# The head of a one-core decoder layer: the values' projection goes first, by rows, and A's chunks run on normed rows

## The chip, the cores and the metric

The kernel runs on one core of one Trainium2 chip. The metric is the device time of one execution in microseconds (us), taken as the median of several runs. Engines are named as in the profile: PE (TensorE's matmuls), PEld (its weight loads), DVE (VectorE), ACT (ScalarE), POOL (GpSimd) and SP (SyncE, which issues nearly all DMAs here).

## The reference

One layer over 256 rows of 1024 channels, all in float32:

```
hn  = rmsnorm(x, norm_mix)                      # per row: x * rsqrt(mean(x^2) + eps) * g
aq, ak, av, bq, bkc, ..., cq, ck, cv, mg = split(hn @ w_in)
o_a = dilated attention of A (6 heads);  o_b = sparse attention of B;  o_c = attention of C
x   = x + (sum of sigmoid(mg) * (o @ w_branch)) @ w_out
x   = x + conv_ffn(rmsnorm(x, norm_ffn));  out = rmsnorm(x, norm_final)
```

Only the first two lines are touched: the norm of `x` and the projections that give A's queries and keys (`aq`, `ak`) and the values `av` of A and `bvs` of B.

## The kernel before, in words

Every large product is made of float32r matmuls on parts: a weight is loaded as `raw` and split into `whi` (a rounded copy, on ACT) and `wlo` (the difference, on DVE or POOL), the activations likewise, and hi*hi, hi*lo and lo*hi are summed in PSUM. Weights come in "units" of up to 128x2048 values (1 MB), in the order of `_unit_list`; each is one DMA on SP's queue (two for the first ones), into one of four `raw` buffers, and its parts go into one of two pairs of `whi`/`wlo` buffers. SP issues in program order and waits at a load whose buffer is still in use.

The work has a head that is written out by hand (`tc.manual_schedule`: ACT, DVE, POOL and PE keep the order of the code), and then a part that a list scheduler orders engine by engine. In the head before:

- `x` is loaded as two tiles of 128 rows, then `table`, then the units a0 and a1 in halves and a2 whole. Nine small matmuls (`keep_warm`, L288) keep PE busy until `x` is there.
- `turn(t)` (L284) transposes x's tile t on PE, 8 blocks of 128x128; both tiles of a block of channels lie side by side, so what is made from `xT` needs both tiles. A small product with `table` (L332) makes the bias table, which goes through DRAM into `T`.
- `hi_part`, `lo_part` (L314, L316, L319) give the parts `x_hi`, `x_lo` of the weighted but not yet normed rows, 256 wide. Chunk c of A's queries and keys (a0, a1, a2 hold two chunks each) is the weights' 128 columns as the stationary operand and `x_hi`/`x_lo` as the moving one: 24 matmuls of 256 columns (L325 for a0, `chunk3_T` L298/L300 for the rest). The row's factor (`rows_m`) is multiplied in afterwards (`by_rows_rstd`, L292).
- Meanwhile ACT and DVE make the normed rows `whole` and their parts `h_parts` (`hn`: hi and lo side by side, 512 wide; L386 to L396), on which everything later works.
- After the head come unit kvc (two chunks by `chunk3_T`, 48 matmuls of 256 columns, L298/L300), then `proj_V("v1")`: rows of h as the stationary operand, the weights (512 columns) as the moving one, 48 matmuls (L238 to L240), copied to `V1` by DVE (L457). Then A's scores (L508) and softmax (L515 to L590), B's queries (`chunk_T`, L426/L428), A's output and so on.

## Time and profile before

| | |
|---|---|
| time, median of 3 runs | 424.87 us (424.62 to 425.62) |
| the profiled execution | 424.76 us, of which the span from first to last instruction is 423.0 |
| PE busy | 412.4 us, 98% of the span |
| DVE, ACT, POOL busy | 313.2 us (74%), 256.2 us (61%), 18.3 us (4%) |
| DMA | 78.00 MB, mean 184 GB/s |
| granted TensorE clock, mean | 0.996 |

Instructions are timed from the start of the span. A row of the timeline gives start, duration, engine, source line, operation, output and input, count, and in brackets how long the engine had been idle before it and what it had waited for. Matmuls overlap: one of 256 columns is shown as some 283 ns long, while the next begins 0.12 us after it, so the pace is read from starts.

### The profile page before, as it was taken

Reading aid. Unit: us, or ns where it says so; the run is one execution under the profiler, and the core shown is the slowest. Engines: PE = TensorE matmul, PEld = TensorE weight load, DVE = VectorE, ACT = ScalarE, POOL = GpSimd, SP = SyncE. Lnnn points to the kernel's source line nnn. Section 1 sums busy time; section 2 is a strip of 40 time slices with the busy share of each in tenths; the row PEclk is TensorE's granted clock in tenths of the full one; section 3 lists DMA queues with packets and bytes.
Section 4 is the critical chain, followed back from the end, with each engine's and each line's share of the span. In section 5 each row is a group of like instructions: output and inputs, shape, how many; then the busy total and the mean of one; then the engine's idle time right before and its main releaser. Section 6 shows DMA issues by size and latency. Waiting matters only on the chain.

```text
span 423.0 us, 6337 instructions
## 1 busy us (share of the span) xinstructions
PE 412.4 (98%) x2407; PEld 347.8 (82%) x2407; DVE 313.2 (74%) x624; ACT 256.2 (61%) x451; POOL 18.3 (4%) x28
## 2 busy tenths in 40 slices
PE   8999999999999999999999999999999999999993
PEld 7998778776667888878788998988888888888883
DVE  3996653788784888434753899998797797887765
ACT  5843283547787855555434889467476576584633
POOL 2500010120000000000000000000000000000001
PEclk9999999999999999999999999999999999999998
DMA  8999419532227793645350465565652743800002
GB/s 279 416 375 407 146 34 354 198 131 100 101 100 248 292 381 109 229 184 198 107 192 0 149 253 198 200 251 200 245 212 105 283 187 110 299 0 2 0 2 99
DMA packets 12750, 78.00 MB, mean 184 GB/s; under 512 B 1408, under 2 KB 1424, under 8 KB 4912
## 3 DMA queue, kind: packets, MB, share of 16 engines
q1 hardware_dynamic: 12144, 75.48, 47.8%
q0 software_dynamic: 576, 2.12, 1.4%
q8 instruction: 19, 0.31, 0.3%
q14 instruction: 11, 0.09, 0.1%
HBM read 76.52 MB, written 1.07 MB: 183 GB/s over the span
## 4 chain that ended last, share of the span: by engine, by line
PE 82%; DVE 8%; ACT 5%; DMA 2%; issue 2%; SPq 0%; POOLq 0%; POOL 0%; ACTq 0%
PE g L988 12%; PE g L239 10%; PE g L240 10%; PE g L238 10%; PE g L990 6%; PE acc L238 6%; PE acc L240 6%; PE acc L239 6%; PE g L298 3%; DVE wlo L226 2%; PE g L888 2%; PE o L541 2%; DMA raw<-in_wts_dram 2%; PE g L426 2%; PE g L300 1%
## 5 line engine op out<-in xcount | busy, mean ns | idle before, releaser
L226 DVE TENSOR_TENSOR wlo<-raw,whi 128x1024 fp32r<-128x1024 f32 (+2 forms) x131 | 154.1, 1201 | 41.0 <-ACT whi L222 40.6
L222 ACT ACTIVATE whi<-raw 128x1024 fp32r<-128x1024 f32 (+2 forms) x130 | 130.2, 1040 | 50.5 <-PE g L240 34.3
L988 PE MATMUL g<-parts,whi 128*128 128x512 f32 x256 | 89.4, 396 | 0.0
L990 PE MATMUL g<-parts,wlo 128*128 128x256 f32 x256 | 66.2, 279 | 0.0
L988 PEld LDWEIGHTS g<-parts,whi 128*128 128x128 f32 x256 | 46.7, 188 | 9.2
L990 PEld LDWEIGHTS g<-parts,wlo 128*128 128x128 f32 x256 | 48.2, 188 | 2.8
L239 PE MATMUL g<-wlo,hn 128*128 128x512 f32 (+1 forms) x128 | 50.0, 391 | 0.0
L240 PE MATMUL g<-whi,hn 128*128 128x512 f32 (+1 forms) x128 | 50.0, 391 | 0.0
L238 PE MATMUL g<-whi,hn 128*128 128x512 f32 (+1 forms) x128 | 49.8, 390 | 0.0
L967 DVE SCALAR_TENSOR_TENSOR cy<-xn,small_b,cy 128x255 f32<-128x255 f32 (+1 forms) x88 | 41.5, 480 | 9.0 <-ACT cy L965 8.0
L238 PE MATMUL acc<-whi,fl 128*128 128x512 f32 (+1 forms) x88 | 34.2, 389 | 0.1
L239 PE MATMUL acc<-wlo,fh 128*128 128x512 f32 (+1 forms) x88 | 34.0, 386 | 0.0
L240 PE MATMUL acc<-whi,fh 128*128 128x512 f32 (+1 forms) x88 | 34.0, 386 | 0.0
L965 ACT ACTIVATE cy<-xn,small_b 128x256 f32<-128x256 f32 x44 | 25.8, 598 | 7.4 <-DVE xn L997 7.4
L239 PEld LDWEIGHTS g<-wlo,hn 128*128 128x128 f32 x128 | 24.1, 188 | 5.1 <-issue 0.9
L240 PEld LDWEIGHTS g<-whi,hn 128*128 128x128 f32 x128 | 24.1, 188 | 4.2 <-issue 0.2
L238 PEld LDWEIGHTS g<-whi,hn 128*128 128x128 f32 x128 | 24.1, 189 | 4.0 <-ACT whi L222 0.2
L426 PE MATMUL g<-hn,whi 128*128 128x512 f32 x72 | 26.2, 405 | 0.0
L996 ACT ACTIVATE xn<-g 128x256 f32<-128x256 f32 x32 | 12.2, 380 | 22.2 <-PE g L988 22.2
L428 PE MATMUL g<-hn,wlo 128*128 128x256 f32 x72 | 19.9, 292 | 0.0
L997 DVE TENSOR_TENSOR xn<-g,xn 128x256 f32<-128x256 f32 x32 | 13.5, 421 | 8.3 <-ACT xn L996 8.3
L240 PEld LDWEIGHTS acc<-whi,fh 128*128 128x128 f32 x88 | 16.5, 188 | 3.4
(213 smaller groups left out, 698.6 us busy)
## 6 DMA issues: line engine op xcount, KB each, us to landing
raw<-in_wts_dram SPq DMA_DIRECT2D x61, 1024.0 KB, 4.8
gl<-in_w_dram SPq DMA_DIRECT2D x8, 512.0 KB, 7.6
raw<-in_wts_dram SPq DMA_DIRECT2D x5, 512.0 KB, 7.4
raw<-in_wts_dram SPq DMA_DIRECT2D x2, 804.0 KB, 9.0
T<-tvd POOLq DMA_DIRECT2D x1, 1280.0 KB, 16.3
xs<-in_x_dram SPq DMA_DIRECT2D x2, 516.0 KB, 3.8
out_dram<-raw SPq DMA_DIRECT2D x4, 256.0 KB, 2.1
T<-tvd POOLq DMA_DIRECT2D x1, 768.0 KB, 9.6
```

The costliest lines, as they stand in the source:

```text
L222: nc.scalar.activation(self.parts[0][:, sl], self.raw[:, sl], AF.Copy)
L226: return (eng or nc.vector).tensor_sub(self.parts[1][:, sl], self.raw[:, sl], self.parts[0][:, sl].bitcast(F32))
L238: nc.tensor.matmul(ps, al, bh, start=start, stop=False)
L239: nc.tensor.matmul(ps, ah, bl, start=False, stop=False)
L240: nc.tensor.matmul(ps, ah, bh, start=False, stop=stop)
L426: hi = lambda: nc.tensor.matmul(ps, view(0, k), h_parts[:, k].rearrange("p a q -> p (a q)"), start=k == 0, stop=k == KC - 1)
L428: lo = lambda: nc.tensor.matmul(ps[:, :S], view(1, k), h_hi[:, k, :], start=False, stop=False)
L965: on_act.append(nc.scalar.activation(y, u, AF.Identity, bias=vec_c[:, 3, ch:ch + 1], scale=vec_c[:, 2, ch:ch + 1]))
L967: nc.vector.scalar_tensor_tensor(y[:, sh:], u[:, :S - sh], vec_c[:, w, ch:ch + 1], y[:, sh:], op0=ALU.mult, op1=ALU.add)
L988: hi = lambda: nc.tensor.matmul(ps, u[0][:, k, cols], h_parts[:, k].rearrange("p a q -> p (a q)"), start=k == 0, stop=k == KC - 1)
L990: lo = lambda: nc.tensor.matmul(ps[:, :S], u[1][:, k, cols], h_parts[:, k, 0, :], start=False, stop=False)
L997: nc.vector.tensor_add(v, ps[:, :S], part)
```

## The change

The values' units v10 and v11 come first. SP loads x's first tile, then the first half of v10, then x's second tile, `table`, the other half of v10, v11, a0, a1, a2. The transposes of a tile are kept together (`turned[t]`: two PSUM tiles of four channel blocks each), so that the first tile's parts need the first tile alone. `weighted` (DVE, from PSUM, with the weights of the norm) writes `whole`, from which ACT makes `raw_hi` and DVE `raw_lo`. `value_products` multiplies rows of the weighted x by the weights, and the row's factor is applied when ACT copies the sums to `V1`. A's six chunks now wait for the normed parts `h_parts` and take 8 matmuls of 512 columns (hi of the weights on hi and lo of h) and 8 of 256 (`chunk_products`), whose halves `chunk_sum` adds. `keep_warm` runs 7 times ahead of the first transposes and 4 times (PAUSE) behind them. `proj_V("v1")` behind kvc is gone. No unit is split on POOL any more.

```diff
-WARM = 9
+WARM = 7
+PAUSE = 4
...
-    out = [(f"a{i}", "w_in", rows, [(C_AQ + 256 * i, 256)]) for i in range(3)]
+    out = [(f"v1{i}", "w_in", [(512 * i, 512)], [(C_AV, 384), (C_BVS, 128)]) for i in range(2)]
+    out += [(f"a{i}", "w_in", rows, [(C_AQ + 256 * i, 256)]) for i in range(3)]
     out.append(("kvc", "w_in", rows, [(C_BKC, 256)]))
-    out += [(f"v1{i}", "w_in", [(512 * i, 512)], [(C_AV, 384), (C_BVS, 128)]) for i in range(2)]
...
     psg = ctx.enter_context(tc.tile_pool(name="psg", bufs=2, space=bass.MemoryType.PSUM))
 
     xs = act_pool.tile([P, NT, D + KC], F32, name="xs")
-    for t in range(NT):
+
+    def load_x(t):
         nc.sync.dma_start(xs[:, t, :], x[t * P:(t + 1) * P, :])
+
+    load_x(0)
...
                 nc.sync.dma_start(self.raw[:, sl], src[:, sl])
+                if between and i == 0:
+                    between()
...
-    turned = [p.tile([P, 512], F32, name=n).rearrange("p (c q) -> p c q", c=2)
-              for p, n in ((ps_t, "t"), (ps_t, "t"), (ps_o, "o"), (ps_o, "o"))]
-    xT = [turned[c // 2][:, c % 2, :] for c in range(KC)]
+
+    whole = [mix.tile([P, 4, S], F32, name="gl", bufs=4) for _ in range(2)]
+
+    turned = [[p.tile([P, 512], F32, name=n).rearrange("p (c q) -> p c q", c=4) for _ in range(2)]
+              for p, n in ((ps_t, "t"), (ps_o, "o"))]
...
 
     T = qkv.tile([P, 16, 256], F32, name="T")
-    u_a0 = Unit("a0", cuts=2)
-    u_a1 = Unit("a1", cuts=2)
-    u_a2 = Unit("a2")
+
+    def load_rest():
+        load_x(1)
+        nc.sync.dma_start(tb, table)
+
+    u_v = [Unit("v10", cuts=2, between=load_rest), Unit("v11")]
     HALF = [slice(n * 512, (n + 1) * 512) for n in range(2)]
-    a0_ps = [psg.tile([P, 512], F32, name="g")[:, :S], s_tile()[:, 0, :S]]
+    V1_ps = [psg.tile([P, 512], F32, name="g"), s_tile()[:, 0, :]]
+    V1 = qkv.tile([P, NT, 512], F32, name="V1")
...
+        def weighted(t, i):
+            nc.vector.tensor_mul(whole[i][:, :, t * P:(t + 1) * P], turned[t][i],
+                                 g_mix[:, 4 * i:4 * i + 4, None].to_broadcast([P, 4, P]))
+
+        def raw_hi_part(t, i):
+            sl = slice(t * P, (t + 1) * P)
+            nc.scalar.activation(raw_hi[:, 4 * i:4 * i + 4, sl], whole[i][:, :, sl], AF.Copy)
+
+        def raw_lo_part(t, i):
+            sl = slice(t * P, (t + 1) * P)
+            nc.vector.tensor_sub(raw_lo[:, 4 * i:4 * i + 4, sl], whole[i][:, :, sl],
+                                 raw_hi[:, 4 * i:4 * i + 4, sl].bitcast(F32))
+
+        def value_products(t, ks, part):
+
             for k in ks:
-                for c, ps in enumerate(a0_ps):
-                    nc.tensor.matmul(ps, u_a0.views[part][:, k, c * P:(c + 1) * P], b[:, k, :],
-                                     start=part == 0 and b is x_hi and k == 0, stop=part == 1 and k == KC - 1)
+                u = u_v[k // 4]
+                for a in (raw_hi, raw_lo)[:2 - part]:
+                    nc.tensor.matmul(V1_ps[t], a[:, k, t * P:(t + 1) * P], u.views[part][:, k % 4, :],
+                                     start=part == 0 and a is raw_hi and k == 0, stop=part == 1 and k == KC - 1)
+
+        def normed_rows(i):
+            nc.vector.tensor_mul(whole[i], whole[i], rows_m[:, None, :].to_broadcast([P, 4, S]))
+
+        def normed_hi(i):
+            nc.scalar.activation(h_parts[:, 4 * i:4 * i + 4, 0, :], whole[i], AF.Copy)
+
+        def normed_lo(i):
+            sl = slice(4 * i, 4 * i + 4)
+            nc.vector.tensor_sub(h_parts[:, sl, 1, :], whole[i], h_parts[:, sl, 0, :].bitcast(F32))
+
+        def chunk_products(u, c):
+
+            ps = psg.tile([P, 512], F32, name="g")
+            cols = slice(c * P, (c + 1) * P)
+            for k in range(KC):
+                nc.tensor.matmul(ps, u.views[0][:, k, cols], h_parts[:, k].rearrange("p a q -> p (a q)"),
+                                 start=k == 0, stop=False)
+            for k in range(KC):
+                nc.tensor.matmul(ps[:, :S], u.views[1][:, k, cols], h_hi[:, k, :], start=False, stop=k == KC - 1)
+            return ps
+
...
+        def chunk_sum(ps):
+            j = len(aT)
+            scale = 0.125 if j < 3 else 1.0
+            part = halves[j % 2][:, :S]
+            nc.scalar.activation(part, ps[:, S:], AF.Copy, scale=scale)
+            aT.append(qkv.tile([P, S], F32, name=f"aT{j}"))
+            nc.vector.scalar_tensor_tensor(aT[j], ps[:, :S], scale, part, op0=ALU.mult, op1=ALU.add)
 
         keep_warm(WARM)
-        rs = [rstd_of([square_mean(xs[:, 0, 0:D], xn[1], "m0")], "m0")]
+        s0 = square_mean(xs[:, 0, 0:D], xn[1], "m0")
         turn(0)
+        for i in range(2):
+            weighted(0, i)
+            raw_hi_part(0, i)
+        keep_warm(PAUSE)
...
+        rs = [rstd_of([s0], "m0")]
+        for i in range(2):
+            raw_lo_part(0, i)
+
+        for i in range(2):
+            u_v[0].hi(i, 4)
+            u_v[0].lo(i, 4)
+        value_products(0, range(2), 0)
         turn(1)
         nc.tensor.matmul(pt[:16, :384], tb[:, R_RB:R_RB + 16], tb[:, R_OH:R_OH + 384], start=True, stop=True)
-
-        for c in (0, 1):
-            hi_part(c, "v")
-        for c in (2, 3):
-            hi_part(c, "a")
-        hi_part(4, "v")
-        split_hi(0, "v")
-        split_hi(1, "a")
-        u_a0.lo(0, 4, nc.gpsimd)
-        u_a0.lo(1, 4, nc.gpsimd)
-        hi_part(5, "v")
-        for c in (6, 7):
-            hi_part(c, "a")
-        split_hi(2, "v")
-        split_hi(3, "a")
-        a0_products(0, x_hi, range(6))
-        ss = square_mean(xs[:, 1, 0:D], xn[1], "m1")
-        for c in range(4):
-            lo_part(c)
-        a0_products(0, x_hi, range(6, KC))
-        a0_products(1, x_hi, range(2))
-        a0_products(0, x_lo, range(3))
-        a0_products(1, x_hi, range(2, 4))
-        u_a0.lo(2, 4, nc.gpsimd)
-        rs.append(rstd_of([ss], "m1"))
+        s1 = [square_mean(xs[:, 1, HALF[0]], xn[1][:, HALF[0]], "m10")]
...
+        raw_hi_part(1, 0)
+        raw_lo_part(1, 0)
+        value_products(1, range(2), 0)
+        for i in (2, 3):
+            u_v[0].hi(i, 4)
+        for t in range(NT):
+            value_products(t, range(2), 1)
+        for i in (2, 3):
+            u_v[0].lo(i, 4)
+        raw_hi_part(1, 1)
+        raw_lo_part(1, 1)
+        s1.append(square_mean(xs[:, 1, HALF[1]], xn[1][:, HALF[1]], "m11"))
+        rs.append(rstd_of(s1, "m1"))
+        for i in range(2):
+            u_v[1].hi(i, 2)
+        for t in range(NT):
+            value_products(t, range(2, 4), 0)
...
+        for i in range(2):
+            u_v[1].lo(i, 2)
+        for t in range(NT):
+            value_products(t, range(2, 4), 1)
...
+        for t in range(NT):
+            value_products(t, range(4, KC), 0)
+        u_a = [Unit("a0")]
         normed_rows(0)
-        by_rows_rstd(2, projected(u_a1, 0))
+        u_a[0].hi(0, 2)
         normed_rows(1)
         normed_hi(0)
+        normed_lo(0)
+        normed_hi(1)
+        normed_lo(1)
+        u_a[0].hi(1, 2)
+        for t in range(NT):
+            value_products(t, range(4, KC), 1)
         for i in range(2):
-            u_a2.lo(i, 2)
-        normed_hi(1)
-        by_rows_rstd(3, projected(u_a1, 1))
-        normed_lo(0)
-        by_rows_rstd(4, projected(u_a2, 0))
-        normed_lo(1)
-        by_rows_rstd(5, projected(u_a2, 1))
+            u_a[0].lo(i, 2)
+
+        for t in range(NT):
+            nc.scalar.activation(V1[:, t, :], V1_ps[t], AF.Copy, scale=rs[t])
+        for n in (1, 2):
+            u_a.append(Unit(f"a{n}"))
+            for i in range(2):
+                u_a[n].hi(i, 2)
+            ps = [chunk_products(u_a[n - 1], 0)]
+            u_a[n].lo(0, 2)
+            chunk_sum(ps[0])
+            u_a[n].lo(1, 2)
+            chunk_sum(chunk_products(u_a[n - 1], 1))
+        for c in range(2):
+            chunk_sum(chunk_products(u_a[2], c))
...
-    V1 = proj_V("v1", 512, "V1")
```

On SP's queue the first rows were, and are (`xs` is x's tiles, `gl` the table's buffer and later those of `w1`, `raw` the weights; 128x1024 is half a unit):

```order
L144 DMA xs<-in_x_dram 128x1032 x2
L270 DMA gl<-in_table_dram 32x784
L217 DMA raw<-in_wts_dram 128x1024 x4
L217 DMA raw<-in_wts_dram 128x2048
L464 DMA small_b<-in_small_b_dram 128x624
```

```order
L146 DMA xs<-in_x_dram 128x1032
L221 DMA raw<-in_wts_dram 128x1024
L146 DMA xs<-in_x_dram 128x1032
L285 DMA gl<-in_table_dram 32x784
L221 DMA raw<-in_wts_dram 128x1024
L221 DMA raw<-in_wts_dram 128x2048 x4
```

Half a unit of weights now stands second, and x's second tile third.

On PE, the head's beginning, before the change (`g` and `s` are the PSUM tiles of a0's two chunks, `t` and `o` those of the transposes):

```order
L288 MATMUL g<-tt 128x128 x9
L284 MATMUL t<-ident,xs 128x128 x4
L284 MATMUL o<-ident,xs 128x128 x4
L284 MATMUL t<-ident,xs 128x128 x4
L284 MATMUL o<-ident,xs 128x128 x4
L332 MATMUL g<-gl 16x384
L325 MATMUL g<-parts,whi 128x256
```

and with it (`g` and `s` now hold the values of the first and the second 128 rows):

```order
L301 MATMUL g<-tt 128x128 x7
L297 MATMUL t<-ident,xs 128x128 x8
L301 MATMUL g<-tt 128x128 x4
L332 MATMUL g<-whi,parts 128x512 x4
L297 MATMUL o<-ident,xs 128x128 x8
L380 MATMUL g<-gl 16x384
L332 MATMUL s<-whi,parts 128x512 x4
L332 MATMUL g<-wlo,parts 128x512 x2
L332 MATMUL s<-wlo,parts 128x512 x2
```

The second tile's transposes and the table's product have moved behind the first four products.

On ACT, the rows between the first square and the first whole halves of a unit, before:

```order
L170 ACTIVATE xn_106,ssm_147<-xs 128x1024
L316 ACTIVATE parts<-t,xs 128x256 x2
L310 ACTIVATE whi<-raw 128x512
L316 ACTIVATE parts<-o,xs 128x256 x2
L310 ACTIVATE whi<-raw 128x512
```

and with the change (`parts` is raw_hi of four channel blocks of one tile):

```order
L174 ACTIVATE xn_106,ssm_138<-xs 128x1024
L320 ACTIVATE parts<-gl 128x4x128 x2
L228 ACTIVATE whi<-raw 128x512 x2
L174 ACTIVATE xn_106,ssm_179<-xs 128x512
L320 ACTIVATE parts<-gl 128x4x128
L228 ACTIVATE whi<-raw 128x512 x2
L320 ACTIVATE parts<-gl 128x4x128
L174 ACTIVATE xn_106,ssm_199<-xs 128x512
```

ACT alone now makes the hi parts, of x and of the weights, which DVE shared before.

## Rows read from the trace of the kernel before

**Rows 1.** The page's first part: the span, and busy time of PE, DVE and ACT with its share of the span and the count of instructions.

```profile
span 423.0 us, 6337 instructions
PE 412.4 (98%) x2407; PEld 347.8 (82%) x2407; DVE 313.2 (74%) x624; ACT 256.2 (61%) x451; POOL 18.3 (4%) x28
```

**Rows 2.** Windows of the head: start and end, length, then busy us (and instructions) of PE, PEld, DVE, ACT and POOL, granted clock, DMA share, GB/s.

```profile
6.50:9.20 2.70, 1.85 (x12) 0.97 (x10) 1.74 (x5) 1.31 (x3) 0.00 (x0) 1.00 0.98 379
9.20:12.00 2.80, 2.35 (x17) 2.15 (x18) 2.34 (x6) 2.80 (x7) 2.76 (x3) 1.00 1.05 430
12.00:15.00 3.00, 3.00 (x27) 3.00 (x27) 3.00 (x9) 3.00 (x6) 1.98 (x3) 1.00 1.00 412
33.40:44.40 11.00, 11.00 (x51) 8.92 (x49) 7.04 (x9) 3.35 (x4) 0.00 (x0) 1.00 0.92 363
```

**Rows 3.** The timeline of the first 11 us: the small matmuls, x's arrival, the transposes, the table's product, the first weights and the first products.

```profile
1.00 3.92 PEld L288 LDWEIGHTS g<-tt 128*128 128x128 f32 x18 [1.00 <-POOL tt L257]
4.07 1.06 ACT L170 ACTIVATE xn<-xs 128x1024 f32<-128x1024 f32 x1 [1.84 <-DMA xs<-in_x_dram]
4.79 0.87 PEld L284 LDWEIGHTS t<-ident,xs 128*128 128x128 f32 x4
5.00 1.06 PE L284 MATMUL t<-ident,xs 128*128 128x128 f32 x4
6.46 0.47 PEld L284 LDWEIGHTS t<-ident,xs 128*128 128x128 f32 x4
7.54 0.81 PE L332 MATMUL g<-gl 32*16 32x384 f32 x2
8.73 0.63 ACT L310 ACTIVATE whi<-raw 128x512 fp32r<-128x512 f32 x1 [0.68 <-DMA raw<-in_wts_dram]
9.22 0.39 PE L325 MATMUL g<-parts,whi 128*128 128x256 f32 x1 [0.86 <-DVE whi L308]
10.87 0.39 PE L325 MATMUL g<-parts,whi 128*128 128x256 f32 x1 [0.43 <-DVE whi L308]
```

**Rows 4.** The chain that ended last, from 14.97 to 45.4 us: start, duration, engine, output, line, count.

```profile
14.97 0.45 PE g L374 x4
16.37 1.92 PE g L298 x16
18.29 0.96 PE g L300 x8
33.65 0.23 PE g L238
43.88 0.23 PE g L238
44.56 0.86 PE s L508 x8
```

**Rows 5.** Groups of instructions by line and shape up to 45 us: line, engine, operation, output and input, shapes, count, busy us, mean ns of one, idle before.

```profile
L226 DVE TENSOR_TENSOR wlo<-raw,whi 128x1024 fp32r<-128x1024 f32 x12 | 14.2, 1217 | 2.5 <-ACT whi L222 2.5
L222 ACT ACTIVATE whi<-raw 128x1024 fp32r<-128x1024 f32 x13 | 13.3, 1056 | 15.3 <-PE g L240 7.8 <-PE g L298 7.5
L389 DVE TENSOR_TENSOR gl<-gl,xn 128x1024 f32<-128x1024 f32 x2 | 2.4, 1210 | 0.0
L457 DVE COPY V<-g 128x512 f32<-128x512 f32 x2 | 1.4, 692 | 1.3 <-PE g L240 1.3
L310 ACT ACTIVATE whi<-raw 128x512 fp32r<-128x512 f32 x2 | 1.3, 632 | 0.7 <-DMA raw<-in_wts_dram 0.7
L226 DVE TENSOR_TENSOR wlo<-raw,whi 128x512 fp32r<-128x512 f32 x1 | 0.7, 671 | 0.0
```

**Rows 6.** How SP issued x's two tiles (start, us of issuing both), the time to landing of x's two tiles, the same of the eight loads of `raw` that SP issued up to 24 us, and windows of 0.5 us (columns as in rows 2; the last two are the DMA engines' busy share and GB/s).

```profile
0.74 0.85 SPq L144 DMA_DIRECT2D xs<-in_x_dram  x2
DMA to landing us min/median/max: 3.3/3.8/4.3
DMA to landing us min/median/max: 6.0/7.8/12.8
4.00:4.50 0.50, 0.50 (x4) 0.50 (x4) 0.00 (x0) 0.43 (x1) 0.00 (x0) 1.00 1.12 421
6.00:6.50 0.50, 0.50 (x5) 0.50 (x4) 0.00 (x0) 0.00 (x0) 0.05 (x1) 1.00 0.70 185
```

**Rows 7.** Windows of A's softmax and of B's, columns as in rows 2.

```profile
53.00:60.00 7.00, 6.87 (x43) 5.66 (x42) 4.12 (x13) 6.57 (x16) 1.47 (x2) 1.00 0.05 20
80.00:90.00 10.00, 9.65 (x66) 7.96 (x64) 8.83 (x30) 5.50 (x10) 3.12 (x3) 1.00 0.58 211
90.00:100.00 10.00, 9.30 (x58) 6.86 (x59) 8.94 (x46) 6.05 (x21) 0.73 (x1) 1.00 0.28 106
100.00:110.00 10.00, 9.65 (x69) 6.48 (x68) 9.39 (x49) 8.34 (x25) 0.74 (x1) 1.00 0.28 105
110.00:120.00 10.00, 9.80 (x73) 6.48 (x71) 8.01 (x45) 8.61 (x27) 0.00 (x0) 1.00 0.01 2
```

**Rows 8.** The bias table's way: POOL issues the two loads of `T`, their time to landing, and A's scores first read it.

```profile
19.34 1.83 POOL L368 DMA_DIRECT2D T<-tvd  x2 [3.90 <-DMA tvd<-tt]
DMA to landing us min/median/max: 9.6/12.9/16.3
46.82 0.29 DVE L515 CUSTOM_DVE_ANT_0 t<-s,T 128x128 f32<-128x128 f32 x1
```

58 lines of the change are left out of this document (7 added, 51 removed).

## The prediction

> **What bounds the kernel now.** I read the busy totals first: PE is busy 98% of the span, DVE 74%, ACT 61% [rows 1], so outside a few places time goes only where PE's work or PE's waits go. Then the windows of the head: PE is busy throughout 12.0 to 15.0 and 33.4 to 44.4, while before that it has holes, 0.85 us in 6.5 to 9.2 and 0.45 in 9.2 to 12.0 [rows 2]. The timeline says what the holes are: x's first tile is there at 4.07, the transposes and the table's product run from 4.8 to 8.35, and the first product starts at 9.22 because the first half of a0 landed only at 8.7; a second wait for split weights ends at 10.87 [rows 3]. After that the chain is PE without a break: the rows' factor at 14.97 (0.45), then 24 matmuls of 256 columns per chunk in 2.88 (16.37 to 19.25 by 1.92 and 0.96) down to 33.65, then 48 matmuls of 512 columns, the 1st at 33.65 and the 46th at 43.88, or 0.227 each, and A's scores at 44.56 [rows 4]. So a change of the head is worth: when PE gets going, what holes follow, and how much PE work is left then. My measure is the moment when A's chunks, kvc and the values are all done: 44.4 on PE's timeline now (the window of rows 2 that ends there, the scores of rows 4 right behind).
>
> **PE's work, old and new.** Old, behind the first product at 9.22: a0's 48 matmuls at 0.12 (5.76), rows' factor 0.45, four chunks 11.52, kvc 5.76, values 48 x 0.227 = 10.9; 34.4 in all. With 9.22 that is 43.6; the other 0.8 are the waits. New: the values' 48 matmuls stay 10.9 (same shape, rows as stationary operand); rows' factor 0.45; kvc 5.76; six chunks of 8 x 0.227 + 8 x 0.12 = 2.78, 16.7 instead of 17.3, so **0.6 less** [rows 4]. The columns streamed per chunk are the same, 24 x 256 = 8 x 512 + 8 x 256; the rows give a matmul of 512 columns less than twice the time of one of 256, and the gain is only that difference. (The Trainium skill, "TensorE: Matmul & The Clock Gate", section "Back-to-back issue gap", prices an isolated matmul at its columns over 2.4 GHz plus 2.5 ns; by it the eight matmuls saved per chunk are worth 0.02 us, 0.1 us in all, and the sum would come out 0.5 us later. Our rows carry about 13 ns per matmul over the columns' time, and I go by them.) Against it, work that PE did while it waited for weights is now behind the first product: the second tile's eight transposes, 8 x 0.12 = 0.95 at the fast pace of 6.46 [rows 3], and the table's product, 0.64 (its 0.81 less the tail). New total 35.5, **1.1 more** than the old behind the first product.
>
> **When the first product can start.** SP now issues half of v10 second, where x's second tile stood, which landed 4.3 after an issue at some 1.2, at 5.5 [rows 6]. But the DMA rate sinks from 421 GB/s at 4.0 to 185 at 6.0 [rows 6], about where the weights begin, so the half unit may take until 7.5; I bound its landing by 5.5 and 7.5. It is not what decides, since ACT and DVE come to it only then. Step by step, with ops of 512 columns at 0.63 on ACT and 0.67 on DVE (0.69 for one out of PSUM) [rows 5]:
> - x's tile at 4.07 as before, its transposes behind the 7 small matmuls (done at 4.05 by 3.92/9 each): results of four blocks 1.27 after the first weight load, as 4.79 to 6.06 now, so 5.4, and the next four at 6.2 [rows 3].
> - `weighted` on DVE 5.4 to 6.1 and 6.2 to 6.9. `raw_hi` on ACT 6.1 to 6.8 and 6.95 to 7.6; then the weights' hi of k=0 to 8.2 and of k=1 to 8.85. DVE makes `raw_lo` by 8.3, in time.
> - PE: two products at **8.3** (0.9 earlier than 9.22), a wait of 0.15, two more to 9.35, the second tile's transposes to 10.3, the table's product to 10.95.
> - Second tile: four blocks ready at 10.1, `weighted` to 10.75, `raw_hi` to 11.45, `raw_lo` (behind the other `weighted` on DVE) to 12.15. So PE waits from 10.95 to 11.5, does one product, waits to 12.2.
> PE's new holes there are 0.55 + 0.45; with the 0.15 that is 1.15, against the old 0.8.
>
> **From 12.2 on PE should not wait again.** 43 of 48 value products (9.8), 0.45, 16.7 and 5.8 are left, 32.7. What it needs comes earlier: hi of k=2,3 by 12.7 on ACT, used at 13.8; v11's hi by 16.2 and lo by 17.6, used at 17 and 20.6. The nearest thing is DVE's queue: v11's lo to 17.6, two `normed_rows` (1.21 each), two `normed_lo` (1.22, as a subtraction of 1024 columns takes), and a0's two lo (1.22) end at 24.95, while PE comes to a0's lo of the upper rows at 24.7 [rows 5]. That is a stall of 0 to 0.25; I take 0.1. a0's lo went to DVE in whole, where POOL had three of its four pieces, and this is its price. V1's copies move from DVE to ACT (1.3 there), whose next use, a1's hi, is due at 28.2 and done at 25.8: nothing. End: 12.2 + 32.7 + 0.1 = **45.0, against 44.4: 0.6 later**.
>
> **What is moved past what.** x's second tile is third in the queue; by bytes it lands where a0's first half did, up to 8.7, and its transposes stand behind 9.35 on PE: hidden, 0.65 in hand. `table`'s product is 2.8 later, so `T` is asked for at about 19.7 instead of 19.34, and the first read of `T` is at 46.8 now, some 43 with the change; the first load of `T` takes 9.6 us, so nothing [rows 8]. a2's load waits for v10's last lo (13.5) and is used at 28; kvc's for v11's (17.6), used at 34; later loads stand behind the four `w1` tiles in SP's queue, whose buffers are free when `normed_lo` is done (22.4). The loads of `raw` take 6.0 to 12.8 here, so these stay hidden too [rows 6]. The scores now stand between kvc's two chunks and in B's first queries instead of among B's queries alone; PE's work is the same.
>
> **Behind the head** the scheduler's order of B's softmaxes and the gates changes in many small places (B's compressed scores come some products earlier). PE's holes there now are 0.13 in 53 to 60 and 0.35, 0.70, 0.35 and 0.20 from 80 to 120, with DVE at 8.0 to 9.4 of 10 [rows 7]: 1.7 in all. That can be won at most, and as much lost; I take nothing.
>
> **Sum.** The profiled execution took 424.76 (span 423.0); 424.76 + 0.6 = **425.4**. The median of the runs is 0.11 above the profiled one, which changes nothing here. What tells a difference from none for this kernel is about 0.2%, 0.85 us.
>
> **Rivals.**
> - *The clock falls back.* At the start PE works at half pace (transposes of 0.21) after 5.4 us of unbroken small work and at the full one (0.12) from 6.46; by its two levels that is 1.2 and then 2.4 GHz, though the granted clock of the windows reads 1.00 [rows 2, 3]. With the change PE is idle from about 7 (four small matmuls behind the transposes) to 8.3 and works half the time until 12.2. (The Trainium skill, "TensorE: Matmul & The Clock Gate", Part 1, says that the array's clock is halved by default and again after idleness; the trace shows the release, and no fall in a hole of 0.86 us.) If it falls, as long a stretch as at the start, 5.4 us, may run at half pace: up to 2.7 lost, of which holes hide 1.0; 1.7 more: 427.1, slower.
> - *The half unit is late.* If v10's first half lands where a0's did, at 8.7, ACT's hi of k=0 ends at 9.35 instead of 8.2 and all behind it moves by 1.1: 426.5, slower. For it: the low rate at 6.0 to 6.5. Against: 1.0 MB stand ahead of its end in the queue, and 1.6 MB of a0's. It decides from a landing past 7.6 on.
> - *B's stage gains from the new order.* If the holes of rows 7 are closed by finer interleaving, up to 1.7 is won back, and a first product some 0.3 sooner adds to it: 425.4 - 2.0 = 423.4, with half of it 424.4; faster from 1.45 of it on. For it: the new order puts scores and transposes more evenly between products. Against: DVE is at 9.4 of 10 there, and order doesn't change its work.
> - *It doesn't do what it says*: the first tile lands no sooner than 4.07, since it was first already. That is in my sum; the only gain at the start is that weights no longer come last.
>
> **How the numbers follow.** Forecast 0.52: from 424.4 to 426.2, of which 0.39 is within 0.2% and 0.13 above. Clock 0.11, all slower. Late weights 0.13, 0.11 of it slower, 0.02 same. B's stage 0.24, 0.22 of it faster, 0.02 same. So faster 0.22, same 0.43, slower 0.35. The range 423.4 to 427.0 leaves out the far ends of the third and the first rival.
>
> **What would show it.** Right: first value product near 8.3, transposes of the second tile behind four products, two holes on PE between 10.9 and 12.2, chunks of 2.78, kvc's last product and the first scores done near 45.9 (45.4 for the values and the scores now). Wrong: transposes of 0.21 behind 9.35 or products of 0.45 (the clock), ACT waiting for `raw` ahead of 8 us (late weights), chunks of 2.9, or PE holes in 80 to 120 us that are far from 1.6.

## The result, and the profile after

The changed kernel takes 427.86 us (median of 6 runs, 427.4 to 428.0) against 424.78 for the kernel before in the same comparison: ratio 1.0067, 95% interval 1.0053 to 1.008. That is 3.1 us slower, where 0.6 was forecast. (In the later comparisons one execution of the kernel before took 582 us and one 510, at mean granted clocks of 0.66 and 0.75; no ratio counts them.) The page of after, first part (span, then busy us, share of the span and instructions of each engine):

```profile
span 426.1 us, 6244 instructions
PE 414.9 (97%) x2363; PEld 345.6 (81%) x2363; DVE 313.5 (74%) x619; ACT 258.5 (61%) x455; POOL 14.7 (3%) x25
```

Against [rows 1] the span grew by 3.1 and PE's busy time by 2.5, though PE runs 44 matmuls fewer: most of the loss is no hole. The timeline of after's first 12 us, which answers [rows 3]:

```profile
4.05 1.06 ACT L174 ACTIVATE xn<-xs 128x1024 f32<-128x1024 f32 x1 [1.81 <-DMA xs<-in_x_dram]
7.33 1.14 ACT L228 ACTIVATE whi<-raw 128x512 fp32r<-128x512 f32 x2
8.00 1.25 PE L332 MATMUL g<-whi,parts 128*128 128x512 f32 x4 [1.07 <-ACT whi L228]
9.08 1.03 PE L297 MATMUL o<-ident,xs 128*128 128x128 f32 x8
10.05 0.81 PE L380 MATMUL g<-gl 32*16 32x384 f32 x2
11.13 0.50 PE L332 MATMUL s<-whi,parts 128*128 128x512 f32 x1 [0.27 <-ACT parts L320]
11.85 0.73 PE L332 MATMUL s<-whi,parts 128*128 128x512 f32 x2 [0.22 <-DVE parts L324]
```

x's first tile comes when it did, ACT turns to v10's first half without waiting for a DMA, and the first product starts at 8.00. The chain that ended last, from A's first chunk on, answers [rows 4] (start, duration, engine, output, line, count):

```profile
22.59 1.84 PE g L350 x8
24.42 0.95 PE g L353 x8
25.38 1.84 PE g L350 x8
...
30.96 1.85 PE g L350 x8
32.82 0.02 issue
32.84 1.07 ACT whi L228
33.91 0.02 issue
33.93 2.36 DVE wlo L232 x2
36.30 0.34 DVE aT L362
36.64 0.04 issue
36.69 2.11 PE g L350 x8
38.80 0.95 PE g L353 x8
39.75 1.92 PE g L307 x16
...
43.48 2.11 PE g L307 x16
45.59 0.97 PE g L309 x8
```

A chunk is 1.84 + 0.95 = 2.79. From 32.84 on the chain leaves PE for ACT and DVE: the split of kvc's weights (L228, L232) stands ahead of the sum of a1's second chunk (aT, L362), which frees the accumulator for a2's second chunk at 36.69. kvc ends at 46.56 with A's first scores (0.86) ahead of its second chunk, so the three are done at 45.7 in the measure of the forecast, against 44.4 before and 45.0 forecast. Windows of after, which answer [rows 7] from 80 to 120 us:

```profile
80.00:90.00 10.00, 9.59 (x66) 7.93 (x66) 9.36 (x29) 4.52 (x8) 1.51 (x2) 1.00 0.30 105
90.00:100.00 10.00, 9.83 (x65) 7.48 (x65) 8.66 (x43) 7.75 (x24) 2.28 (x2) 1.00 0.49 179
100.00:110.00 10.00, 9.26 (x65) 6.08 (x65) 9.03 (x48) 8.37 (x25) 0.74 (x1) 1.00 0.16 54
110.00:120.00 10.00, 9.63 (x77) 6.09 (x78) 7.70 (x46) 7.82 (x30) 0.00 (x0) 1.00 0.21 86
```

PE's holes are 1.69 us there, against 1.60 before. Where both programs have the same matmuls left to issue, their starts give the delay exactly: 1.09 us when the kernel before is at 52 us, 1.67 at 130, 3.08 at the last matmul. Behind 128 us both programs issue the same 1542 matmuls in the same order, and still the delay grows from 1.7 to 3.1 us, in steps of hundredths. The timeline of PE shows it: the first and last of the same 31 matmuls of 512 columns, in the kernel before,

```profile
168.49 0.39 PE L239 MATMUL g<-wlo,hn 128*128 128x512 f32 x1
...
175.29 0.39 PE L239 MATMUL g<-wlo,hn 128*128 128x512 f32 x1
```

and in the changed one:

```profile
170.36 0.39 PE L245 MATMUL g<-wlo,hn 128*128 128x512 f32 x1
...
177.35 0.39 PE L245 MATMUL g<-wlo,hn 128*128 128x512 f32 x1
```

Thirty steps take 6.80 and 6.99 us, 0.2267 and 0.2329 each, with PE busy throughout and the granted clock at 1.00. Counted from the starts of all such matmuls between 130 and 240 us, 11% go at the slower pace before (over 0.2285) and 60% after. This percentage is called the share below.

### The profile page after: what moved, and what is told of

Same layout as the page of the kernel before. It is cut to its first block, busy times and chain, and to the rows that moved or that the text cites. A ratio compares the mean times of both kernels' runs of the same rounds, so it can differ in the third digit from the quotient of the medians.

```text
span 426.1 us, 6244 instructions
## 1 busy us (share of the span) xinstructions
PE 414.9 (97%) x2363; PEld 345.6 (81%) x2363; DVE 313.5 (74%) x619; ACT 258.5 (61%) x455; POOL 14.7 (3%) x25
## 2 busy tenths in 40 slices
DMA packets 12605, 77.99 MB, mean 183 GB/s; under 512 B 1392, under 2 KB 1408, under 8 KB 4640
## 4 chain that ended last, share of the span: by engine, by line
PE 87%; DVE 7%; ACT 4%; issue 1%; POOL 0%; POOLq 0%; ACTq 0%
PE g L1012 14%; PE g L244 9%; PE g L246 9%; PE g L245 9%; PE g L1014 7%; PE acc L244 6%; PE acc L245 6%; PE acc L246 6%; PE g L452 2%; PE g L350 2%; DVE wlo L232 2%; PE g L912 2%; ACT tt L583 1%; PE g L332 1%; PE s L332 1%
## 5 line engine op out<-in xcount | busy, mean ns | idle before, releaser
L232 DVE TENSOR_TENSOR wlo<-raw,whi 128x1024 fp32r<-128x1024 f32 (+2 forms) x134 | 156.0, 1189 | 46.2 <-ACT whi L228 45.7
L228 ACT ACTIVATE whi<-raw 128x1024 fp32r<-128x1024 f32 (+2 forms) x134 | 132.2, 1027 | 43.9 <-PE g L246 26.9
L244 PE MATMUL g<-whi,hn 128*128 128x512 f32 (+1 forms) x112 | 44.0, 394 | 0.0
L246 PE MATMUL g<-whi,hn 128*128 128x512 f32 (+1 forms) x112 | 43.8, 391 | 0.0
L245 PE MATMUL g<-wlo,hn 128*128 128x512 f32 (+1 forms) x112 | 43.8, 391 | 0.0
L246 PE MATMUL acc<-whi,fh 128*128 128x512 f32 (+1 forms) x88 | 34.1, 388 | 0.0
L244 PEld LDWEIGHTS g<-whi,hn 128*128 128x128 f32 x112 | 21.0, 188 | 4.4 <-issue 0.8
L245 PEld LDWEIGHTS g<-wlo,hn 128*128 128x128 f32 x112 | 21.1, 188 | 4.2 <-issue 0.3
L246 PEld LDWEIGHTS g<-whi,hn 128*128 128x128 f32 x112 | 21.1, 188 | 3.8
## 6 DMA issues: line engine op xcount, KB each, us to landing
T<-tvd POOLq DMA_DIRECT2D x1, 768.0 KB, 10.3
```

Of the source, the lines that this page charges most:

```text
L228: nc.scalar.activation(self.parts[0][:, sl], self.raw[:, sl], AF.Copy)
L232: return (eng or nc.vector).tensor_sub(self.parts[1][:, sl], self.raw[:, sl], self.parts[0][:, sl].bitcast(F32))
L244: nc.tensor.matmul(ps, al, bh, start=start, stop=False)
L245: nc.tensor.matmul(ps, ah, bl, start=False, stop=False)
L246: nc.tensor.matmul(ps, ah, bh, start=False, stop=stop)
```

## Experiments: is the pace the program's, and where does the attention stage lose?

Two controls, both kernels unchanged, and two single edits of the kernel before.

> The kernel before, unchanged, profiled once more. In its first trace the 512-column products ran at two paces, 0.2266 us or about 0.2335 us from one start to the next; of those between 130 and 240 us 11% had the slower one, after the change 60%. If the pace belongs to the program (theory 1), this second trace shows the share near 10% again and a span near 423 us. If it is chance of each execution (theory 2), the share may be anything between 10% and 70%, and the span moves with it by up to 1.4 us.

> The changed kernel, unchanged, profiled once more. Theory 1 (the slower pace of the 512-column products belongs to the program): about 60% of those between 130 and 240 us take about 0.2335 us again, span near 426 us. Theory 2 (chance of each execution): the share differs from the first trace by more than 20 points, in one of the two controls at least. The head is to repeat in both theories: kvc's second product ends near 46.5 us.

Shares of slow matmuls in 130 to 240 us: 12% and 58%, and matmul by matmul nearly the same pattern as in the first traces (93% of the matmuls before and 96% after are at the same pace in both). So the pace is the program's. c_before itself took 427.05; its windows (columns as in rows 2) say why:

```profile
8.00:10.00 2.00, 0.03 (x1) 0.03 (x1) 0.51 (x2) 0.51 (x1) 0.00 (x1) 1.00 1.01 410
10.00:12.00 2.00, 1.56 (x11) 1.36 (x12) 1.51 (x4) 2.00 (x5) 2.00 (x2) 1.00 1.06 438
12.00:14.00 2.00, 2.00 (x13) 2.00 (x12) 2.00 (x7) 2.00 (x4) 2.00 (x3) 0.54 0.99 417
14.00:16.00 2.00, 2.00 (x13) 2.00 (x13) 2.00 (x5) 1.85 (x5) 0.94 (x2) 0.61 1.04 420
```

a0's first half came 0.75 later than in [rows 3], PE waited 2.16 us for it (7.81 to 9.97), and from 12 to 16 us the granted clock is near half. The delay is 2.24 us at 16 us and stays so. Of 100 executions of the kernel before in the five later comparisons 29 took 426 us or more, 26 of these with a mean granted clock of 0.991 to 0.994; those with 0.995 or more have medians of 424.8 to 424.9. Neither trace of the changed kernel shows a clock under 1.00 there.

```diff
+    h_parts = act_pool.tile([P, KC, 2, S], F32R, name="hn")   # moved ahead of xn
     xn = [act_pool.tile([P, D], F32, name=f"xn{t}") for t in range(NT)]
```

> The kernel before with one difference: the normed rows' tile is allocated ahead of the two scratch tiles for x, as in the changed kernel, so these lie at other addresses; no instruction is added, removed or moved. Theory 1a (the slower pace comes from where the tiles lie): about 60% of the 512-column products between 130 and 240 us at the slower pace, and the time 1.0 to 1.4 us above before (about 426). Theory 1b (it comes from another part of the program) and theory 2 (chance): time within 0.4 us of before, share near 10% by 1b.

425.54 us, ratio 1.001 (0.9992 to 1.0028), share 11%: by the share, since the interval of the time is wide, theory 1a falls for this tile.

```diff
+    V1 = proj_V("v1", 512, "V1")
     u = unit("kvc")
```

> The kernel before with the values' projection ahead of the key and value chunks for the compression (kvc), so that A's first scores stand right behind kvc as in the changed kernel; the head is as before. Theory 3 (the 0.6 us that the changed kernel loses between 46 and 128 us come from this order): 0.4 to 0.8 us slower than before, with the loss in this stretch. Theory 4 (they come from the stall of A's last chunk or from the sums and are only carried there): the time within 0.3 us of before. The share of slow products in 130 to 240 us should stay near 10% by theory 1a.

425.0 us, ratio 1.0003 (0.9986 to 1.002); against the first trace of before it is 0.19 us ahead up to 28 us, 0.06 late at 52 and still 0.06 late at 128. The order of kvc and values alone costs 0.25 us at most, and nothing behind 52 us: theory 3 falls.

## Experiments: 32 bytes

The changed kernel has one column tile more among the small ones (a second sum of squares for x's second tile). It takes 32 bytes per partition and moves every pool behind it, while the first weight buffers and the normed rows keep their place to a multiple of 8192 bytes. Before, the tiles of weights and activations that these matmuls read all begin at 192 modulo 256 bytes; with the column those behind it begin at 224.

```diff
+    small.tile([P, 1], F32, name="pad", bufs=1)
     wpools = [(wpool, 4, 2)]
```

> The kernel before with one unused column tile more in the pool of small tiles, which moves every pool behind it by 32 bytes, as the changed kernel's one more sum of squares does; no instruction is added or moved. Theory A (the slower pace is set by addresses: a 512-column product takes about 0.2335 us instead of 0.2266 us where its moving operand and the weights that are loaded beside it begin in different 32-byte halves of a 64-byte line, since so it reads in the first two traces, 98% slow where they differ and 17 to 47% where they don't): the share of slow ones between 130 and 240 us goes from 11% to about 60%, and the time up by 1.2 to 1.6 us, to about 426.2. Theory B (the pace comes from the changed kernel's instructions or their timing): share near 11%, time within 0.3 us of before.

Share 60%, time 426.02 us (ratio 1.0017, 1.0004 to 1.0031), and the same 31 matmuls at the changed kernel's pace (timeline of PE):

```profile
168.28 0.39 PE L240 MATMUL g<-wlo,hn 128*128 128x512 f32 x1
...
175.27 0.39 PE L240 MATMUL g<-wlo,hn 128*128 128x512 f32 x1
```

From 130 us to the end it loses 1.38 us against before, where the changed kernel loses 1.41; ahead of it, it gains 0.4. The cause is the 32 bytes. What about them, three pads in the changed kernel told (one column, 24 and 56 columns):

> The changed kernel with the same unused tile, so that the pools lie 64 bytes further than before the change in place of 32; no instruction differs. Theory A: the share of slow 512-column products between 130 and 240 us falls from 60% to 10 to 20%, the time by 1.2 to 1.6 us, to about 426.4; if the attention stage (46 to 128 us) loses its 0.6 us for the same reason, by up to 2.0, to 425.9. Theory B: time stays within 0.3 us of 427.9.

> The changed kernel with an unused tile of 96 bytes in the pool of small tiles, so that all pools lie 128 bytes further than before the change, in place of 32; no instruction differs. Over the five kernels traced so far, a 512-column product followed by another was slow in 25% of 3110 cases where its moving operand and the next weights begin at the same place of a 128-byte line, and in 78 to 98% where they don't (32, 64 and 96 bytes apart), which is why moving by 64 gave back only 0.2 us. Theory A (the address within 128 bytes sets the pace): the share of slow ones between 130 and 240 us falls to 10 to 20%, the time by 1.1 to 1.5 us against the changed kernel, to about 426.5. Theory B (the first layout was special in some other way): share near 50 to 60%, time 427.3 to 427.9.

Neither expectation held: 427.63 us with a share of 52%, 427.82 with 54%. (The second one's time is no clean measure: in its trace ACT waits 1.7 us for a weight unit near 150 us, and 0.9 us of the delay arises there.)

> The changed kernel with an unused tile of 224 bytes in the pool of small tiles, so that all pools lie 256 bytes further than before the change; no instruction differs. Sorted anew, over eight traced kernels, a 512-column product followed by another was slow in 27% of 3871 cases where moving operand and next weights begin at the same place of a 256-byte line, in 90% of 624 where they lie 128 bytes apart, and in 68 to 98% at 32, 64, 192 and 224; so a move by 128, tried before, could not help. Theory A (the address within 256 bytes sets the pace): share of slow ones between 130 and 240 us back at 10 to 20%, time 1.1 to 1.5 us under the changed kernel's, about 426.5. Theory B (something else of the layout): share near 55%, time above 427.3.

426.35 us (425.73 to 426.7) and a share of 12%; the same 31 matmuls:

```profile
169.67 0.39 PE L246 MATMUL g<-wlo,hn 128*128 128x512 f32 x1
...
176.48 0.39 PE L246 MATMUL g<-wlo,hn 128*128 128x512 f32 x1
```

6.81 us again. So by medians 1.5 of the 3.1 us are the layout's. The changed kernel and this one issue the same matmuls in the same order; matmul by matmul this one gains 1.47 us behind 130 us and 0.26 between 12 and 28 us, in the head, where the slow part of the value and chunk products falls from 80% to 38%. Over 17 traces, for matmuls behind 128 us, by the distance from the start of the moving operand to that of the weights loaded for the next matmul, taken from the tiles' addresses in the program, modulo 256 bytes:

```
512 columns, then 512:   0: 9561 matmuls, 23% slow, mean 0.2280 us     32: 524, 98%, 0.2332
                        64: 350, 98%, 0.2332     128: 624, 90%, 0.2324
                       192: 428, 68%, 0.2292     224: 294, 97%, 0.2331
256 columns, then 256:   0: 4017, mean 0.1193 us     32: 720, 0.1183     64: 294, 0.1178
                        96: 142, 0.1174     128: 189, 0.1190     224: 173, 0.1171
```

With 512 columns equal places are fast, with 256 columns they are slow, and there 128 bytes apart too. The changed kernel's first trace alone says the same: between 130 and 240 us 29% of 237 matmuls at equal places are slow, and 99% of 179 at 32 and 224 bytes. Two tests of the second half were spoiled by my own edits, both made before the period of 256 was known:

```diff
-    h_raw = act_pool.tile([P, KC, 2, S], F32R, name="hn")
+    h_raw = act_pool.tile([P, KC * 2 * S + 16], F32R, name="hn")[:, 8:KC * 2 * S + 8]
```

> The kernel before with the tile of normed rows 64 bytes longer, and its second use (as the moving operand of the feed-forward's first products) begun 32 bytes into it, so that there, and only there, moving operand and weights lie in different halves of a 64-byte line; no instruction is added or moved. The traces so far show 256-column products followed by 256-column ones at 0.1194 us where the halves are the same (470) and 0.1182 us where they differ (148). If the address also sets the pace of these: 0.2 to 0.5 us faster than before. If that difference came from something else: time within 0.15 us of before.

424.99 us (ratio 0.9997, 0.9982 to 1.0012). In the trace it gains 0.25 us between 240 and 280 us, where the edit works, and loses 0.3 between 132 and 240, since the longer tile put the weights 64 bytes from the normed rows (share 44%). As a test of time it decides nothing.

## Experiments: the head and kvc's split

```diff
-            chunk_sum(chunk_products(u_a[n - 1], 1))
+            ps = chunk_products(u_a[n - 1], 1)
+            if n == 2:
+                u_k = Unit("kvc")
+                u_k.hi(0, 2)
+            chunk_sum(ps)
+        u_k.hi(1, 2)                     # then u_k.lo, behind a2's first products
```

> The kernel of the run just before (changed, pools 64 bytes on) with the split of kvc's weights written into the order by hand: its first high half ahead of the sum of a1's second chunk on the scalar engine, the rest behind that sum. In the changed kernel the whole split stands ahead of the two halves of this sum, and a2's second chunk starts at 36.69 instead of 36.4 because its accumulator waits for the sum. Theory: 0.3 to 0.5 us faster than the kernel without this edit, kvc's first product at about 39.2 instead of 39.59. Rival (the 0.3 us are given back in the attention stage, which waits for other work): time within 0.2 us of that kernel.

427.4 us against 427.63 without the edit, 0.23 less by medians: between theory and rival. The traces tell more, since both kernels issue the same matmuls in the same order: the edited one is 0.52 us late up to 36 us, because its first product came later in that execution, and 0.12 from 36.5 us to the end. The edit gains 0.40 us at that one place, and nothing is given back: the theory.

> The changed kernel with all pools 256 bytes on and the split of kvc's weights in the order by hand, its products where the change has them: what is left of the change without its two side effects. The first was worth 1.5 us in the median, the second 0.2 to 0.4 where the layout was another. Theory: the two add up, 425.9 to 426.2, still 1.0 us or more slower than before, of which 0.7 to 0.8 between 46 and 128 us (attention). Rival (they overlap, since both let A's last chunk start earlier): 426.2 to 426.5.

425.83 us (12 runs), 0.5 under a_align256 by medians, and 0.40 by the traces: matmul by matmul 0.46 late up to 32 us, by the start of that execution, and 0.06 from 36.5 us on. So they add up. Against the kernel before the ratio is 1.0009 (0.9995 to 1.0024); it is 0.95 us above the median of those 13 of its 22 executions there with a mean granted clock of 0.995 or more. a2's two chunks in a_align256, and here with the sum on ACT between them and kvc behind:

```profile
33.08 2.00 PE L351 MATMUL g<-hn,whi 128*128 128x512 f32 x8
36.17 2.11 PE L351 MATMUL g<-hn,whi 128*128 128x512 f32 x8
```
```profile
33.54 2.00 PE L351 MATMUL g<-hn,whi 128*128 128x512 f32 x8
33.75 0.37 ACT L361 ACTIVATE xn<-g 128x256 f32<-128x256 f32 x1
36.33 2.00 PE L351 MATMUL g<-hn,whi 128*128 128x512 f32 x8
39.12 2.08 PE L308 MATMUL g<-hn,whi 128*128 128x256 f32 x16
```

The sum's ACT half is done at 34.1 instead of 35.1 in the changed kernel, and the step to a2's second chunk takes 2.79 instead of 3.09 us; the other 0.1 us is that chunk's first product. Where the same matmuls are left, this kernel is 0.63 us behind the kernel before at 52 us, 1.24 at 130 and 1.22 at the end: what is left arises in the head and in the attention stage.

```diff
-    load_x(0)
+    for t in range(NT):
+        load_x(t)
...
-    u_v = [Unit("v10", cuts=2, between=load_rest), Unit("v11")]
+    u_v = [Unit("v10", cuts=2), Unit("v11")]
```

> The changed kernel with its load order undone: both tiles of x and the table ahead of the values' weights, as before. If the order of loads is worth what the head's working says, the first value product moves from 8.0 to 9.1 to 9.4 us and the head's end by 0.5 to 1.2 us; time about 428.6. If the second tile's work then fills the wait (its transposes stand behind the first products in TensorE's queue, so I doubt it): within 0.3 us of the changed kernel. Sums and layout are as in the changed kernel, so the share of slow products should stay at 60%.

430.79 us (ratio 1.0117, 1.0089 to 1.0146): 2.9 us worse than the changed kernel, more than expected. Its windows:

```profile
8.00:10.00 2.00, 0.49 (x2) 0.30 (x2) 0.68 (x2) 1.17 (x3) 0.00 (x0) 1.00 1.05 434
10.00:12.00 2.00, 2.00 (x11) 1.79 (x10) 1.04 (x3) 0.60 (x2) 0.00 (x0) 0.64 1.03 434
12.00:14.00 2.00, 2.00 (x6) 0.41 (x4) 1.84 (x4) 1.53 (x3) 0.00 (x0) 0.50 1.00 422
14.00:16.00 2.00, 2.00 (x5) 1.61 (x6) 2.00 (x5) 2.00 (x5) 0.10 (x1) 0.50 0.95 401
```

The first product starts at 9.51 after a wait of 2.0 us, 1.5 us later than in the changed kernel, and then the granted clock is at half, 0.50 for 4 us. Matmul by matmul the delay to the changed kernel is 1.5 us at the first products, 3.8 at 14 us, and stays so. Three of the four runs (430.66 to 431.69) have mean granted clocks of 0.989 to 0.993; the fourth took 428.87 at 0.995, a clock that the changed kernel's runs have too. So, as far as that one run tells, the order of loads by itself is worth some 1.0 us, near what was expected, and the fall of the clock that came with the longer wait another 1.8 to 2.8.

## Experiment: the attention stage

```diff
-    u = u_k.views                        # kvc's products and sums, ahead of A's scores
     for g in range(3):                   # A's scores
...
+    u = u_k.views                        # the same, behind them
```

> The changed kernel with all pools 256 bytes on, the split of kvc's weights in the order by hand, and kvc's products written behind A's scores in place of ahead of them, so that the scheduler orders the attention stage anew; the work is the same. The kernel before and the changed one do the same work there in another order, and the changed one takes 0.6 us more. Theory (the stage's length is that of the order the scheduler happens to choose): it differs from that of the changed kernel by 0.3 us or more, either way. Rival (the 0.6 us come from the sums of A's chunks, which are as in the changed kernel): the same delay to the kernel before at 128 us as in the changed kernel with the split in order, 1.45 us, within 0.2.

427.03 us. Two points at which all these kernels have the same matmuls left bound the stage: 52.30 and 130.02 us in the kernel before. Between them lie the following windows (columns as in rows 2), before, changed, and a256_order:

```profile
52.30:130.02 77.72, 76.00 (x542) 57.07 (x540) 55.10 (x218) 50.20 (x133) 6.79 (x8) 1.00 0.39 142
53.39:131.69 78.30, 76.48 (x542) 57.15 (x540) 53.89 (x208) 49.98 (x133) 6.73 (x8) 1.00 0.40 150
52.80:130.79 77.99, 76.28 (x541) 57.42 (x540) 54.57 (x208) 49.16 (x131) 6.54 (x9) 1.00 0.41 149
```

The same work takes 77.72, 78.30 (78.32 in a256_kvc, which lacks the shift) and 77.99 us: the other order gives back 0.31 of the 0.6 us, just what the theory asked for, where the rival had the whole loss stay. PE's holes are 1.72, 1.82 and 1.71, so most of the difference lies in what the profile shows as busy: waits that a matmul's modelled end covers. From 48.6 us on, the steps from a projection's product of 512 columns to a transpose, a score or an attention output that take over 0.34 us number 4 before (1.08 us above 0.32 each), 10 after (2.63) and 5 here (1.11). So the scheduler's order is worth 0.3 us, and these waits go with it; that they are the cause, and where the other 0.3 us come from, is not shown. The total does not show the gain, for two reasons. Ahead of this stretch, with the new order, A's second scores wait until DVE has read the first ones (m, L534):

```profile
43.31 0.93 PE L527 MATMUL s<-aT,aT 64*128 64x128 f32 x8 [0.72 <-DVE m L534]
```

And near 150 us ACT waits 2.5 us for a weight unit, where b_warm (below) waits too; 1.7 us of the delay arise there.

## Experiments: can the kernel before be made faster with this?

```diff
+        for _ in range(10):
+            nc.tensor.matmul(pt[:, 384:], idle, idle, start=True, stop=True)
```

> The kernel before with ten 128-column products on zeros behind the table's product, in the wait of TensorE for the first half of a0's weights (7.9 to 9.2 us in one trace, 7.8 to 10.0 in the other). In the second trace of the kernel before this wait was 2.16 us, the granted clock fell to 0.54 and 0.61 in the two stretches of 2 us from 12 to 16 us, and the execution took 2.2 us more, 0.75 of it by the first product. Theory (the other 1.4 us are the clock's): executions of 426 us and more, a quarter of those of the kernel before, disappear, the longest near 425.6; the median falls by 0 to 0.4 us. Rival (the products on zeros don't hold the clock, or hold up the head): the upper group stays, or the median rises by 0.2 us or more.

> The kernel before with the ten products on zeros of the run just before this, and with two tiles begun 32 bytes further: x's parts in the head and the normed rows in the feed-forward's first products, both moving operands of 256-column products; all other tiles keep their place in a 128-byte line. In the traces so far 256-column products followed by such took 0.1192 us where moving operand and next weights begin at the same place of a 128-byte line (1206 cases, 82% over 0.1185) and 0.1168 to 0.1183 us where they don't (756 cases). If that is the address: 0.4 us less in the head (as in the kernel before moved by 32 bytes, which ran ahead by 0.43 us at 40 us) and 0.3 to 0.4 us less in the feed-forward layer, so 0.6 to 0.9 us less than the run just before, about 424.0. If not: the time of that run within 0.2 us.

Both missed. b_warm took 426.12 us (ratio 1.0022, 1.0008 to 1.0035). The clock's part of the theory held: all 12 runs have a mean granted clock of 0.996 to 0.998. But it is level with before up to 132 us, then 1.35 us late by 184. The waits of ACT from 128 to 185 us have a line that the kernel before lacks:

```profile
ACT whi L222 <- DMA raw<-in_wts_dram: 1.6, 1, 1.6
```

The weight unit issued at 144.2 us in both kernels is split from 150.6 on instead of 148.9, in a stretch (142 to 154 us) where the DMA engines are 0.93 to 0.99 busy. Why it lands later is not shown. b_best took 427.35 us: a like wait (1.2), and a share of 66%, since its tiles were 128 bytes longer and put weights and normed rows half a period apart; the head's 256-column products ran at 0.1173 us instead of 0.1199, as expected. With 256 bytes:

```diff
-    raw_parts = mix.tile([P, KC, 2, S], F32R, name="parts")
+    raw_parts = mix.tile([P, KC * 2 * S + 64], F32R, name="parts")[:, 8:KC * 2 * S + 8]
```

> The kernel before with the tile of x's parts 256 bytes longer and its first use, as the moving operand of the head's 256-column products, begun 32 bytes into it; everything else keeps its place in a 256-byte line. Where moving operand and next weights begin at the same place, 256-column products followed by such took 0.1192 us in the traces so far (1392 cases), at a distance as here 0.1171 (161). If the address sets this: about 190 products of the head by 0.0023 us, 0.4 us faster, about 424.4, and the share of slow 512-column products stays at 10 to 15%. If not: within 0.15 us of before.

424.29 us against 424.91, ratio 0.9994 (0.9982 to 1.0006); 0.47 us ahead of before from 28 us on (about half of it by 16 us), and nothing changes behind the head. With six products on zeros, once and then again:

> The kernel of the run just before with six products on zeros in TensorE's wait for a0's first weights, where ten were tried without that layout: those took away the executions with the clock at half, but a weight unit landed 1.6 us late at 150 us, where the DMA engines are full, in what seems every execution. If that late landing is luck of the timing: no executions above 426 us, median 424.3 to 424.6, under the kernel before. If anything that moves TensorE's program by a few instructions brings it: 1.0 to 1.4 us slower than the run just before.

> The same kernel as two runs before (kernel before, x's parts 32 bytes further in a tile 256 bytes longer, six products on zeros), once more, since its gain is near what one comparison can tell: 424.2 to 424.6 in the median if the gain of 0.4 to 0.5 us is real, with at most one execution in ten above 426; 424.7 to 425.0 if it was the draw of the executions.

424.42 us (ratio 0.9991, 0.998 to 1.0002), then 424.4 (0.9977, 0.9965 to 0.999). None of the 23 runs took over 425.8 or has a mean granted clock under 0.995, and ACT waits for no weight unit in either trace. So by medians this version is 0.4 and 0.5 us faster than the executions of the kernel before whose clock did not fall (424.8 and 424.88 in the two comparisons), and the group with the fallen clock is gone besides. The whole gain, 0.1 and 0.2%, is clear of noise in the second comparison alone. That ten products bring the late unit and six don't is measured in two traces of each, not explained; a_align128 and a256_order have a late unit without any.

## Why the prediction was wrong

- **The first product and the holes: right.** Forecast 8.3, second tile's transposes 9.35, table's product 10.3, products at 11.5 and 12.2; measured 8.00, 9.08, 10.05, 11.13 and 11.85, with every gap between them within 0.12 us of what was worked out. From there PE is full, as said, up to 36 us. The half unit was not late, and the clock did not fall: these rivals did not come. Their prices, 1.1 and 1.7, were fair: in a_xfirst a first product 1.5 us later costs 1.0, and the fall of the clock 1.8 to 2.8 more, by one run against three. [rows 3] showed no fall after a hole of 0.86 us; c_before and a_xfirst show one after 2.16 and 2.0. (The Trainium skill, "TensorE: Matmul & The Clock Gate", Part 1, has the clock halved again after idleness; these two traces agree, with 0.54 and 0.50.)
- **The chunks: right.** 2.79 against 2.78; the saving of 0.6 is there. The total of new work has a slip without effect: 33.8 + 0.95 + 0.64 is 35.4, 1.0 more than the old, not 35.5 and 1.1; the 45.0 doesn't rest on it.
- **kvc's split: the step that was missing in the head.** I checked the splits inside the order written by hand, and took kvc's for hidden because its load was. It was the scheduler's to place, and it went ahead of the sum that frees an accumulator of which there are two, so that a2's second chunk waited: 0.40 us by the edit's two traces. The three were done at 45.7 instead of 45.0, although the products were 0.35 ahead at 11.85. Beside the split, 0.26 of that is the layout's (below), and 0.2 is kvc's second chunk, 3.08 instead of 2.88: A's scores now stand on either side of it. It is not the split's, since the chunk takes 3.06 in a256_kvc too. The other 0.2 is not broken down.
- **"I take nothing" behind the head: the step that failed most.** I looked for waits and holes, and took 0.227 us per matmul of 512 columns as given, since the matmuls are the same. A tile of one column, which no term of the sum had, moved operands by 32 bytes and made half of these matmuls 3% slower: 1.5 us by medians, more than half of the 2.5 by which the forecast missed.
- **The attention stage: the sign was open, and it went against.** The rival had holes closing by up to 1.7; they stayed (1.69 against 1.60), and still 0.6 us were lost between 52 and 130 us. The order that the scheduler chose is worth 0.3 of it, as a256_order shows. Short waits between projection products and softmax work go with it, which the holes of [rows 7] do not show because a matmul's modelled end covers them; that they are the cause, and what the other 0.3 is, stays open.

In sum, by medians: 427.86 with all, 426.35 without the shift, 425.83 without shift and split, 424.9 before. By the trace, the miss of 2.5 is 0.5 up to 52 us (1.09 late, 0.6 forecast), 0.6 from there to 130 us and 1.4 behind it. Without its two side effects the change costs about 0.9 us, near the 0.6 forecast. Part of that nearness is luck, since the attention stage, taken at nothing, is 0.6 of it; and the forecast was for the kernel as it was, with a range that ended at 427.0.

## What to carry to other kernels

When a change adds or removes a tile, however small, compare the operands' addresses as well as the instructions: here 3% on half of the large matmuls of the last 300 us cost more than three times what kvc's split did. An order written by hand protects only what stands in it: a unit whose split is left to the scheduler can land ahead of what frees an accumulator, as kvc's did. Compare two traces matmul by matmul where the programs issue the same ones: executions of these kernels start their first products up to 0.8 us apart, which hid a gain of 0.40 in the totals. And watch the waits at the start of PE's work: undoing the load order cost 2.9 us, of which some two thirds seem to be the clock's, which fell after a wait of 2.0 us.

## What the runs showed of the hardware

The rate of back-to-back matmuls depends on where the moving operand lies against the next weights within 256 bytes: 0.2280 us on the mean for 512 columns at equal places, 0.2331 to 0.2332 at 32, 64 and 224 bytes, and the other way round for 256 columns, 0.1193 against 0.1171 at 224 (but 0.1190 at 128). (The Trainium skill, "SBUF — State Buffer", section "A bandwidth-pool intuition that's wrong (but worth ruling out)", lists a second, independent read port for loading weights beside the moving operand's; by that alone one would not expect the place to matter, the runs show that it does, and the measurement decides.) The mechanism behind it is not shown by any run here. That the addresses are the cause is shown for 512 columns, by four pads that move tiles and change no instruction: 32 bytes in the kernel before bring the slow pace, 224 in the changed one (256 with its own column) take it away, 32 and 96 (64 and 128) don't. For 256 columns it rests on the table and on b_parts256, whose 0.47 us lie in the trace of the head.
